# Hymba block on one core: a rule for each product of a head, rotary tables in other buffers, mixes stored from ScalarE's queue, two norm roots moved ahead

## The chip, the cores and the metric

The kernel runs on one core of a Trainium2 chip. A core has five engines with instruction queues of their own: TensorE (PE in the profile, PEld its weight loads), VectorE (DVE), ScalarE (ACT), GpSimd (POOL) and SyncE (SP). In this kernel nearly all transfers between HBM and on-chip memory are issued by SP. The metric is the time of one execution in microseconds of device time, the median of several runs.

## The reference, cut to what matters

One layer over 1040 tokens (16 learned meta tokens and 1024 of input) of width 1024, in float32: a token mixer with eight heads, then a gated MLP with a causal depthwise convolution. Heads 0 to 3 are mLSTM heads (convolved q and k, exponential gates, a carried state), heads 4 to 7 retention heads (rotary q and k, a fixed decay). Each head's output is normalised, gated and projected.

```python
def token_mixer(u, w_in, ml_conv_w, ml_b_i, ml_b_f, ml_norm_g, rt_norm_g, w_out):
    proj = up @ w_in
    (ml_q, ml_k, ml_v, ml_o, ml_i, ml_f, rt_q, rt_k, rt_v, rt_g) = jnp.split(proj, offs, axis=-1)
    qk = jax.nn.silu(causal_dwconv(jnp.concatenate([ml_q, ml_k], axis=-1), ml_conv_w))
...
    h_ml = mlstm_chunkwise(to_chunks(q), to_chunks(k), to_chunks(v),
                           to_chunks(li[..., None])[..., 0], to_chunks(lf[..., None])[..., 0])
    h_ml = head_norm(from_chunks(h_ml), ml_norm_g).reshape(b, lp, ML_HEADS * ML_DV)
    h_ml = jax.nn.sigmoid(ml_o.astype(jnp.float32)) * h_ml
    rq = rotary(rt_q.astype(jnp.float32).reshape(b, lp, RT_HEADS, RT_DQK), pos)
...
    h_rt = retention_chunkwise(to_chunks(rq), to_chunks(rk), to_chunks(rv), log_gamma)
    h_rt = head_norm(from_chunks(h_rt), rt_norm_g).reshape(b, lp, RT_HEADS * RT_DV)
    h_rt = jax.nn.silu(rt_g.astype(jnp.float32)) * h_rt
    mixed = jnp.concatenate([h_ml, h_rt], axis=-1).astype(u.dtype)
    return (mixed @ w_out)[:, n_pad:]

        h = h + token_mixer(rmsnorm(h, norm_mix_g[l]), w_in[l], ml_conv_w[l], ml_b_i[l], ml_b_f[l],
                            ml_norm_g[l], rt_norm_g[l], w_out[l]).astype(h.dtype)
        h = h + channel_mixer(rmsnorm(h, norm_ffn_g[l]), w_up[l], w_gate[l], ffn_conv_w[l],
                              w_down[l]).astype(h.dtype)
    return rmsnorm(h, norm_final_g)[:, N_META:]
```

## The kernel before

**Products.** Activations lie with features on the 128 partitions and tokens along the free side. Every large product is computed with seven block products instead of eight (a Winograd form): `ROWS` lists the seven with the activation block that each uses, "11" to "22" and the sums S1 to S4. Each operand is split into a rounded high half and a low rest (`hi`, `lo`), and three matmuls at the fast float32 format stand for one product (`mm3s`, L858 to L860). So each weight block needs a cast on ACT (L440) and a subtraction on DVE (L445) before PE can use it (`parts`). The sequential part, the scan of a head, uses plain float32 matmuls.

**Start (to about 90 us).** `norm_sums` and `norm_split` normalise the input in five pieces: squares on ACT and DVE, sums on PE (L786), a root on ACT (L788), a reciprocal on DVE (L789), a broadcast on PE (L798), the scaling on DVE (L837) and the split (L838, L842). Meanwhile PE computes v, q and k of head 4 and the gate columns. Then DVE and ACT build S1 to S4 and split them (`usplit`, L1722 and L1723). For S4 the block "12" is first copied by POOL to the tiles `x12` (L1743), since its own place becomes that of S4's low half. `x12` has the tags A1 and A2; the tables of the heads (rotary cosine and sine, or the mLSTM weights) have the same tags, so `tables_load(4)` (L1053, L1054) has to wait until S4 is split.

**The planned stage (about 80 to 720 us).** The program walks through the products of the heads in the order 4, 0, 1, 2, 3, 5, 6, 7: q and k (`qk_steps`), v for pairs of heads (`v_steps`), the output gate (`o_steps`). `slot` emits one step of a product and, between steps, side tasks from the list `side`, in order. Side tasks of a head are the convolution or the rotary turn (`qk_tasks`), the tables (`tables_tasks`), nine pairs of `scan_a` (score product L1465, transposition L1470, then pt on DVE at L1484 or L1489 and kw on ACT at L1481) and `scan_b` (state update u at L1513, output n at L1515, C on DVE, norm statistics), and for three pieces of the tokens `post_steps`: `stats`, and two times `half`, which transposes into the one bank tr (L1573), multiplies into `mx` (L1581) and stores it to `mxd` in HBM from SP (L1594). `mx` has three buffers.

Many tasks are generators: `tick` advances those in `pend` (weights being split) and `front` (side tasks under way), and emits deferred evacuations. A cost model in `watch` keeps a clock for each engine (`load`) and the end of each instruction (`fin`); tasks wait until the model says that their input is ready (`done.can`, `settle`, `landed`). A step emits at most two side tasks, at most one of them with PE work, and none while DVE or ACT is more than 2.5 us ahead of PE in the model; weights up to three units ahead of the running product (`near`) are split first. With `pinned` set, the order written so is the order on PE, DVE and ACT; transfers are placed by the framework's scheduler, which has an estimate of its own.

**Weights.** `jput` loads raw weights from SP as soon as one of four slots is free; a slot is freed when its last block has been split. `w_unit` adds up blocks of the output weights on DVE (L601 to L605) for later; `first_right` reads mixes back from `mxd` and splits them for the first output product.

**Hand-over.** After the last gate product (`o_steps(7)`) the output product `mixw` starts, with its first weights split by `mixw.prep` (L742 on ACT, L743 on DVE), between the last chunks of head 7's scan.

```python
near = [g for g in pend if order.get(owner[id(g)], 10 ** 6) <= cursor[0] + 3]
for q in (near, front, pend):
...
    if q is pend and not rush[0] and max(load["DVE"], load["Activation"]) - load["PE"] > 3:
        break
    if not rush[0] and until[id(g)] > load["PE"] + 0.5:
        continue
```

## Time and profile before

| what | value |
|---|---|
| median of 3 runs (lowest, highest) | 1569.39 us (1566.6, 1570.87) |
| the profiled execution's own time | 1569.85 us |
| its span, first to last instruction | 1567.6 us |
| mean granted clock of PE | 0.984 |
| moved by DMA | 223.80 MB, mean 143 GB/s |

The profile is that of one execution. Its page gives busy times of engines, the span in 40 slices, the DMA queues, the chain of work that ended last, and the costliest groups of instructions. Other views of the same trace list waits (who waited for whom), instructions in order of time, and busy time and granted clock by stretch. An instruction is named by its line in the kernel, its engine and its tiles, output before input; x is a count. Busy time of PE is that of pipelined matmuls whose ends are modelled, so a busy PE is not PE at its peak. "<-" names what ended a wait, inferred from semaphores.

### The profile page before, as it was taken

To read this page: it belongs to the slowest core of one execution; us is meant where nothing else is said; L and a number is where in the kernel's file an instruction comes from. 1 tells how busy PE (TensorE), PEld (TensorE's weight loads), DVE (VectorE), ACT (ScalarE), POOL (GpSimd) and SP (SyncE) were. 2 spreads that over 40 slices of the span, in tenths; PEclk is the share of its full clock that TensorE was granted. 3 is DMA by queue.
4 is the path that set the end of the run, shared out by engine and by line. 5 is a ranking of instruction groups with operands and counts; after the bars stand their busy time and mean duration, and the time that the engine had idled before them with its cause. 6 is when DMAs were issued, how large, how long until landed. Compare 5 with 4: busy or idle time off the path is not lost.

```text
span 1567.6 us, 25461 instructions
## 1 busy us (share of the span) xinstructions
PE 1503.6 (96%) x9929; PEld 1362.7 (87%) x9929; DVE 1092.4 (70%) x2107; ACT 757.7 (48%) x1454; POOL 73.3 (5%) x133
## 2 busy tenths in 40 slices
PE   7979998999999998999999999999999999999997
PEld 6969888899989898997887988999999999888887
DVE  7775677667676767684777778766666666678657
ACT  5355545445555454655344556444444444434443
POOL 1000000000000000000000000222220000000000
PEclk8989999999999999999999999999999999999999
DMA  6022245323632246569542417788873223943313
GB/s 226 1 82 55 81 135 189 108 72 102 191 103 94 89 135 202 171 248 349 201 122 81 148 54 226 215 208 198 210 180 99 77 76 104 387 134 101 97 52 108
DMA packets 104585, 223.80 MB, mean 143 GB/s; under 512 B 10520, under 2 KB 33760, under 8 KB 104288
## 3 DMA queue, kind: packets, MB, share of 16 engines
q1 hardware_dynamic: 95872, 199.02, 38.0%
q0 software_dynamic: 8448, 23.07, 7.3%
q8 instruction: 78, 1.28, 0.3%
q14 instruction: 43, 0.35, 0.1%
q10 hardware_dynamic: 144, 0.07, 0.0%
HBM read 178.05 MB, written 67.15 MB: 156 GB/s over the span
## 4 chain that ended last, share of the span: by engine, by line
PE 87%; DVE 7%; DMA 3%; ACT 2%; issue 1%; SPq 0%; DVEq 0%; ACTq 0%
PE pdx L860 3%; PE pdx L859 3%; PE pdx L858 3%; PE pup_x L859 2%; PE pup_x L860 2%; PE pga_x L858 2%; PE pup_x L858 2%; PE pga_x L859 2%; PE pga_x L860 2%; PE n L1515 2%; PE pdy L860 2%; PE pdy L859 2%; PE pdy L858 2%; PE u L1513 2%; PE pv L898 2%; PE pwx L860 2%
## 5 line engine op out<-in xcount | busy, mean ns | idle before, releaser
L742 ACT CAST hi_up<-raw_up 128x512 fp32r<-128x512 f32 (+1 forms) x52 | 36.4, 719 | 107.1 <-PE pga_z L859 60.6
L743 DVE TENSOR_TENSOR lo_ga<-fraw_ga,hi_ga 128x512 fp32r<-128x512 f32 (+1 forms) x52 | 41.9, 808 | 38.7 <-ACT hi_ga L742 38.6
L858 PE MATMUL pup_x<-uh_g,hi_up 128*128 128x256 f32 (+1 forms) x240 | 67.2, 283 | 1.2 <-ACT uh_g L1857 1.2
L743 DVE TENSOR_TENSOR lo_up<-raw_up,hi_up 128x512 fp32r<-128x512 f32 (+1 forms) x52 | 41.3, 810 | 38.2 <-ACT hi_up L742 37.4
L859 PE MATMUL pup_x<-ul_g,hi_up 128*128 128x256 f32 (+1 forms) x240 | 67.4, 282 | 0.1
L860 PE MATMUL pup_x<-uh_g,lo_up 128*128 128x256 f32 (+1 forms) x240 | 66.4, 282 | 0.0
L743 DVE TENSOR_TENSOR lo_d<-rd,hi_d 128x1024 fp32r<-128x1024 f32 (+1 forms) x34 | 37.7, 1113 | 32.8 <-ACT hi_d L742 32.7
L742 ACT CAST hi_ga<-fraw_ga 128x512 fp32r<-128x512 f32 (+1 forms) x52 | 36.4, 719 | 46.3 <-PE pup_z L859 23.4
L860 PE MATMUL pdx<-uh_d,lo_d 128*128 128x512 f32 (+1 forms) x156 | 57.9, 375 | 0.0
L859 PE MATMUL pdx<-ul_d,hi_d 128*128 128x512 f32 (+1 forms) x156 | 57.8, 374 | 0.0
L742 ACT CAST hi_d<-rd 128x1024 fp32r<-128x1024 f32 (+1 forms) x34 | 32.3, 959 | 49.2 <-PE pdy L859 32.5
L860 PE MATMUL pdy<-uh_d,lo_d 128*128 128x512 f32 x132 | 51.9, 393 | 0.0
L859 PE MATMUL pdy<-ul_d,hi_d 128*128 128x512 f32 x132 | 51.7, 392 | 0.0
L858 PE MATMUL pdx<-uh_d,hi_d 128*128 128x512 f32 (+1 forms) x156 | 48.5, 372 | 0.0
L858 PE MATMUL pdy<-uh_d,hi_d 128*128 128x512 f32 x132 | 47.9, 389 | 0.0
L858 PE MATMUL pga_x<-uh_g,hi_ga 128*128 128x512 f32 x120 | 47.5, 396 | 0.0
L859 PE MATMUL pga_x<-ul_g,hi_ga 128*128 128x512 f32 x120 | 47.5, 396 | 0.0
L858 PEld LDWEIGHTS pup_x<-uh_g,hi_up 128*128 128x128 f32 x240 | 45.3, 189 | 2.3 <-ACT uh_g L1857 1.4
L860 PE MATMUL pga_x<-uh_g,lo_ga 128*128 128x512 f32 x120 | 47.1, 393 | 0.0
L859 PEld LDWEIGHTS pup_x<-ul_g,hi_up 128*128 128x128 f32 x240 | 45.4, 189 | 1.0 <-DVE ul_g L1858 0.3
L860 PEld LDWEIGHTS pup_x<-uh_g,lo_up 128*128 128x128 f32 x240 | 44.8, 189 | 0.8
L1581 DVE SCALAR_TENSOR_TENSOR mx<-tr,vec,sig 128x386 f32<-128x386 f32 (+2 forms) x42 | 24.0, 572 | 26.0 <-PE tr L1573 17.0
(1684 smaller groups left out, 5789.7 us busy)
## 6 DMA issues: line engine op xcount, KB each, us to landing
raw_up<-w_up_d SPq DMA_DIRECT2D x22, 512.0 KB, 4.4
fraw_ga<-w_gate_d SPq DMA_DIRECT2D x22, 512.0 KB, 4.6
acts<-cv SPq DMA_DIRECT2D x44, 256.0 KB, 4.3
wsd<-w_down_d POOLq DMA_DIRECT2D x44, 256.0 KB, 6.3
rd<-wsd SPq DMA_DIRECT2D x22, 512.0 KB, 3.5
raw_w<-w_out_d SPq DMA_DIRECT2D x20, 512.0 KB, 5.1
wsw<-raw_w SPq DMA_DIRECT2D x32, 256.0 KB, 2.1
raw_m<-w_out_d SPq DMA_DIRECT2D x14, 512.0 KB, 3.7
```

The source lines that it names most:

```text
L742: AC.copy(hi[:, o:o + n], x)
L743: V.tensor_tensor(lo[:, o:o + n], x, hi[:, o:o + n].bitcast(F32), ALU.subtract)
L858: m.append(PE.matmul(pt, ah, xh_, start=first and k == 0, stop=False, skip_group_check=True))
L859: PE.matmul(pt, ah, xl_, start=False, stop=False, skip_group_check=True)
L860: m.append(PE.matmul(pt, al, xh_, start=False, stop=last and k == n - 1, skip_group_check=True))
L898: PE.matmul(pv[:, :nv], u[:, kb % 4, j0:j0 + L], (w0hi, w0lo)[j][kb // 4][:, o:o + nv], start=i + j + kb == 0, stop=i == 1 and kb == KB - ...
L1513: PE.matmul(up[:, :nv], kw[:L], v, start=True, stop=True)
L1515: PE.matmul(pn[:L, :nv], pt[:L, :L], v, start=True, stop=c == 0)
L1581: return V.scalar_tensor_tensor(dst, tr[:, x0 - t0:x1 - t0], vec[:, g:g + 1], sig(b, p)[:, x0 - a0:x1 - a0], ALU.mult, ALU.mult)
```

## The change

- **Rules.** A table `RULES` gives each product (kind and head) seven numbers: how many units ahead weights count as near; how far ahead of PE a generator's input may be; at what lead of DVE or ACT the rest of `pend` pauses; the same limit for side tasks; how many of these in a step; which of three orders the queues have; how many of them may have PE work. `RULE` holds for the others. Side tasks that start on PE go to a new queue, `hot`.
- **Model.** A DMA from ACT is priced apart from SP's; a change between the two matmul formats costs 0.1 in the model; `done["tr"]` is set after the mix has been emitted and not before; `scan_a` waits for the one before it, `scan_b` for the evacuation of its values; the stage starts with DVE 7.0 and ACT 5.5 behind, before 4.0 and 2.0.
- **Tables.** `x12` takes the tags v2 and v3; `tables_load(4)` stands ahead of the copies and of S4.
- **Stores.** `half` stores the mix from ACT's queue, after `settle`; `first_right` waits until all three pieces of its mix are stored.
- **Memsets.** The ones in `mv`, `den` and `vz` are written by POOL, in `scan_a` of the first chunk.
- **Norms.** Squares and casts are ordered behind the last root, and a sum behind the last reciprocal.
- **Hand-over.** `mixw.pump` and `mixw.prep(0)` come before the last steps of `o_steps(7)`; the next `prep` after the first quarter of each product.

```diff
+RULE = (3, 0.5, 3.0, 2.5, 2, 0, 1)
+RULES = {
+    ("o", 0): (4, 0.3, 3.0, 2.5, 2, 0, 3),
+    ("o", 1): (3, 0.0, 2.0, 1.5, 2, 1, 3),
...
+    ("vp", 2): (3, 0.3, 3.0, 4.0, 2, 1, 2),
+}
...
-            load[eng] = t + 0.4
+            load[eng] = t + (0.4 if eng == "SP" else 0.1)
...
+                whole = F32 in [x.dtype for x in ins.ins]
+                c += 0.1 * (whole != kindof[0])
+                kindof[0] = whole
...
-        near = [g for g in pend if order.get(owner[id(g)], 10 ** 6) <= cursor[0] + 3]
-        for q in (near, front, pend):
+        near = [g for g in pend if rank.get(owner[id(g)], 10 ** 6) <= cursor[0] + rule[0][0]]
+        for q in ((hot, near, front, pend), (near, hot, front, pend), (hot, front, near, pend))[rule[0][5]]:
...
-                if q is pend and not rush[0] and max(load["DVE"], load["Activation"]) - load["PE"] > 3:
+                if q is pend and not rush[0] and max(load["DVE"], load["Activation"]) - load["PE"] > rule[0][2]:
                     break
-                if not rush[0] and until[id(g)] > load["PE"] + 0.5:
+                if not rush[0] and until[id(g)] > load["PE"] + rule[0][1]:
                     continue
...
             def g():
+                while not {(k, x) for x in range(3)} <= stored:
+                    yield
                 ask([i])
...
-        V.reciprocal(col[:, :ns], col[:, :ns])
+        last["recip"] = V.reciprocal(col[:, :ns], col[:, :ns])
...
-        AC.activation(sq[0], xs[0], AF.Square)
+        m = AC.activation(sq[0], xs[0], AF.Square)
+        if r:
+            after(m, last["sqrt"])
...
-            AC.activation(sq[1], xs[1], AF.Square)
+            after(AC.activation(sq[1], xs[1], AF.Square), last["sqrt"])
...
-            V.tensor_tensor(sq[0], sq[0], sq[1], ALU.add)
+            m = V.tensor_tensor(sq[0], sq[0], sq[1], ALU.add)
+            if r:
+                after(m, last["recip"])
...
-            AC.copy(w0hi[i], w0raw[i])
+            after(AC.copy(w0hi[i], w0raw[i]), last["sqrt"])
...
+        if c == 0:
+            mv = mxp.tile([P, 4, 2], F32, tag="mv", name=f"mv{h}_0", bufs=4)
+            den = mxp.tile([P, NCH], F32, tag="den", name=f"den{h}", bufs=2)
+            G.memset(mv[:, 0, :], 1.0)
+            G.memset(den[:, 0:1], 1.0)
+            if h < H:
+                G.memset(vz[:META, VZ[h] * 264 + DV:VZ[h] * 264 + VW], 1.0)
+            firsts[h] = mv, den
...
-                V.memset(mv[:, 0, :], 1.0)
-                V.memset(state["den"][:, 0:1], 1.0)
-                if h < H:
-                    V.memset(vz[:META, VZ[h] * 264 + DV:VZ[h] * 264 + VW], 1.0)
...
+            done.discard("tr")
             tr = ps.tile([P, 512], F32, tag="tr", name=f"tr{h}_{p}_{b}")
...
-            done["tr"] = fin[0] + 0.05
...
             mix_into(mx[:, :w], a0, t1)
+            done.add("tr")
             e = min(t1, MB + HB)
-            nc.sync.dma_start(mxd[i][:, a0 - MA:e - MA], mx[:, :e - a0])
             if e < t1:
                 V.tensor_copy(mm[:, i], mx[:, e - a0:w])
                 posted.add(i)
+            yield from settle()
+            AC.dma_start(mxd[i][:, a0 - MA:e - MA], mx[:, :e - a0])
+            stored.add((i, p))
...
-            return lambda: done.can(("qk", h, int(c > 4)), *([("tab", h)] if h < H else ["gates"] if h == 4 else [])) and not (h == 7 and "meta" in done)
+            return lambda: done.can(*([("pre", h, c - 1)] if c else []), ("qk", h, int(c > 4)), *([("tab", h)] if h < H else ["gates"] if h == 4 else [])) and not (h == 7 and "meta" in done)
...
-            spawn(g, front)
+            spawn(g, hot if pe else front)
...
+        if key:
+            rule[0] = RULES.get(key[:2], RULE)
+        lim, most = rule[0][3:5]
+        pe = max(pe, rule[0][6])
...
-    x12 = [st.tile([P, 2 * SB], F32, tag=f"A{i + 1}", name=f"s4_{i}").rearrange("p (k j) -> p k j", k=2) for i in range(2)]
+    x12 = [vslot(2 + i, f"s4_{i}").rearrange("p (k j) -> p k j", k=2) for i in range(2)]
+    tables_load(4)
     for i in range(2):
         G.tensor_copy(x12[i], part("12", i))
     s1[:] = x12
     need(("o", 4, 1))
     usplit("S4", "S1", "uh2", "ul2")
-    tables_load(4)
...
-    load.update({"DVE": 4.0, "Activation": 2.0})
+    load.update({"DVE": 7.0, "Activation": 5.5})
...
-    go(steps[4:])
+    go(steps[4:12])
+    issue(len(units) - len(fu))
+    while ("o", 7, 6) not in done:
+        slot(steps[10 + used[0]])
+        used[0] += 1
+    mixw.pump()
+    mixw.prep(0)
+    go(steps[12 + used[0]:])
...
     for t in range(KW - 2):
-        for u in (t, t + 1):
-            mixw.prep(u)
+        mixw.prep(t)
         for j in range(4):
             slot(lambda: mixw.mms(t, js=(j,)))
+            if j == 0:
+                mixw.prep(t + 1)
```

More of the change, by code (lines that the diff above doesn't have):

```diff
@@ L133, in watch @@
         if dma:
[L134 removed]
+            load[eng] = t + (0.4 if eng == "SP" else 0.1)
             size = n * o.ap[0][1] * 4e-6
[L136 to L137 removed]
+            if eng == "SP":
+                load["wire"] = max(load["wire"], t + 1.8) + size / 0.3 * (2 if "scr" in str(rd) else 1)
+                end = load["wire"]
+            else:
+                load["wire"] += size / 0.3
+                end = t + 1.8 + size / 0.15
         else:
@@ L340, in body @@
     front = []
+    hot = []
     evacs = []
@@ L345, in body @@
     cursor = [0]
+    rule = [RULE]
     def spawn(g, q=pend, key=None):
@@ L363, in tick @@
     def tick():
-        assert pend or evacs or front
+        assert pend or evacs or front or hot
         fin[0] = 0.0
@@ L410, in flush @@
         rush[0] = True
-        while pend or evacs or front:
+        while pend or evacs or front or hot:
             tick()
@@ L455, in issue @@
             ready[u[0]] = u[2]()
-    order = {}
+    order, rank = {}, {}
     place = {}
@@ L463, in need @@
             order.update({u[0]: i for i, u in enumerate(units)})
-        i = i0 = cursor[0] = order[key]
+            rank.update({k: i for i, k in enumerate(u[0] for u in units if u[1])})
+        i = i0 = order[key]
+        cursor[0] = rank[key]
         if ahead is None:
@@ L1018, in step, with out @@
                     bank = bank.rearrange("p (c j) -> p c j", j=DV)
-                    defer(lambda: evac(n, d, bank))
+                    f, half = QUAD[n]
+                    key = ("v", (a, b)[f], half) if cp == 3 and n in (1, 4, 5, 6) else None
+                    def out():
+                        evac(n, d, bank)
+                        if key:
+                            done.add(key)
+                    defer(out)
                 step.key = "vp", p, n
@@ L1500, in scan_b @@
         if slot == 0:
-            mv = mxp.tile([P, 4, 2], F32, tag="mv", name=f"mv{h}_{p}", bufs=4)
             if p == 0:
-                state["den"] = mxp.tile([P, NCH], F32, tag="den", name=f"den{h}", bufs=2)
-                V.memset(mv[:, 0, :], 1.0)
-                V.memset(state["den"][:, 0:1], 1.0)
-                if h < H:
-                    V.memset(vz[:META, VZ[h] * 264 + DV:VZ[h] * 264 + VW], 1.0)
+                mv, state["den"] = firsts.pop(h)
+            else:
+                mv = mxp.tile([P, 4, 2], F32, tag="mv", name=f"mv{h}_{p}", bufs=4)
             outs[p] = ([], mv, state["den"])
@@ L1603, in ra @@
         def ra(c):
-            return lambda: done.can(("qk", h, int(c > 4)), *([("tab", h)] if h < H else ["gates"] if h == 4 else [])) and not (h == 7 and "meta" in done)
+            return lambda: done.can(*([("pre", h, c - 1)] if c else []), ("qk", h, int(c > 4)), *([("tab", h)] if h < H else ["gates"] if h == 4 else [])) and not (h == 7 and "meta" in done)
         turn = [("vm", p, s) for p, x in enumerate(PAIRS) for s in range(2) if x[s] == h]
         def rb(c):
-            return lambda: (h, c) in pre and done.can(("pre", h, c), *(turn if c == 0 else [("n", h, c - 1)]))
+            v = [("v", h, int(c > 4))] if h not in (4, 7) else []
+            return lambda: (h, c) in pre and done.can(("pre", h, c), *(turn if c == 0 else [("n", h, c - 1)] + v))
         A = [(lambda c=c: scan_a(h, c), 1, ra(c)) for c in range(NCH)]
```

19 lines of the change are left out of this document (10 added, 9 removed), and 16 rows, old and new, of the table RULES.

## The prediction

> **What bounds the kernel now.** The page comes first: the span, the engines' shares and part 4, the chain that ended last (PE is TensorE, PEld its weight load, DVE VectorE, ACT ScalarE, POOL GpSimd).
>
> ```profile
> span 1567.6 us, 25461 instructions
> ...
> PE 1503.6 (96%) x9929; PEld 1362.7 (87%) x9929; DVE 1092.4 (70%) x2107; ACT 757.7 (48%) x1454; POOL 73.3 (5%) x133
> ...
> PE 87%; DVE 7%; DMA 3%; ACT 2%; issue 1%; SPq 0%; DVEq 0%; ACTq 0%
> ```
>
> PE is the bound: it holds 87% of the chain, and the change removes no product. What can be won is where PE stood still (1567.6 - 1503.6 = 64 us) or ran at a low clock. The next view is the busy time in stretches; columns are the stretch, its length, busy PE, PEld, DVE, ACT and POOL, the granted clock, the DMA share and GB/s.
>
> ```profile
> 80.00:120.00 40.00, 29.79 (x228) 27.99 (x229) 29.07 (x73) 20.82 (x41) 0.21 (x2) 0.87 0.25 82
> 120.00:720.00 600.00, 572.94 (x4405) 539.20 (x4404) 409.47 (x938) 310.46 (x652) 8.91 (x42) 0.98 0.43 139
> 720.00:760.00 40.00, 36.29 (x167) 28.00 (x166) 25.45 (x47) 19.99 (x30) 0.00 (x0) 1.00 0.88 329
> ```
>
> Three stretches matter beside the norms at the front: the start of the first gate product (80 to 120; PE idle 10.2 us), the planned stage (120 to 720; idle 27.1 us), and its hand-over to the output product (720 to 760; idle 3.7 us). The change touches nothing behind. DVE is busy 68% of the planned stage (409.47 of 600), so it is late in places and not short as a whole. The list of PE's waits says for whom (total us, times, longest):
>
> ```profile
> PE po4y L858 <- DVE sig L930: 8.4, 1, 8.4
> ...
> PE s L1465 <- DVE pt L1489: 6.4, 2, 4.1
> PE u L1513 <- DVE vz L1507: 6.2, 4, 3.0
> PE tr L1573 <- DVE mx L1581: 4.8, 6, 1.8
> PE po1y L860 <- DVE lo_o L445: 2.9, 1, 2.9
> ...
> PE po1x L860 <- DVE lo_o L445: 1.8, 1, 1.8
> ```
>
> Each long wait is also followed by PE at half clock for some microseconds. The same view of stretches, cut around the dips:
>
> ```profile
> 24.00:36.00 12.00, 10.16 (x50) 10.08 (x50) 11.88 (x30) 5.26 (x10) 0.00 (x0) 0.58 0.15 57
> 92.00:108.00 16.00, 9.05 (x55) 8.84 (x56) 11.48 (x33) 11.67 (x20) 0.00 (x0) 0.68 0.20 71
> 196.00:208.00 12.00, 9.02 (x45) 7.31 (x45) 9.53 (x21) 4.73 (x11) 0.18 (x1) 0.72 0.52 176
> ...
> 372.00:380.00 8.00, 8.00 (x53) 7.52 (x53) 7.12 (x12) 2.74 (x6) 0.17 (x1) 0.79 0.19 68
> ```
>
> Length times (1 - clock) is what a dip takes: 5.0, 5.1, 3.4 and 1.7 us; in the second, half falls into the idle time itself, so I count 2.6.
>
> **The change part by part.**
>
> *Rotary tables in free buffers.* The copies of x12 leave the tiles A1 and A2 for v2 and v3, and the loads of the tables come ahead of them. The timeline of DVE, SP's queue and PE (start, length, instruction, count, and in brackets the idle time before it and what ended that):
>
> ```profile
> 74.09 2.43 DVE L1723 TENSOR_TENSOR uS1l<-s,uS1h 128x1056 fp32r<-128x1056 f32 x2 [0.81 <-ACT uS1h L1722]
> ...
> 83.86 2.42 DVE L1723 TENSOR_TENSOR uS4l<-s,uS4h 128x1056 fp32r<-128x1056 f32 x2
> ...
> 86.15 0.38 SPq L1053 DMA_DIRECT2D A<-rot_d  x1
> ...
> 91.55 0.71 DVE L1131 TENSOR_TENSOR qT<-rawq,A 128x528 f32<-128x528 f32 x1 [5.27 <-DMA A<-rot_d]
> ...
> 94.38 0.71 DVE L1132 TENSOR_TENSOR kT<-kT,A 128x528 f32<-128x528 f32 x1 [2.12 <-DMA A<-rot_d]
> ...
> 98.95 0.58 PE L858 MATMUL po4y<-uS1h,hi_o 128*128 128x256 f32 x1 [8.38 <-DVE sig L930]
> ```
>
> The tables now go out at 86.15, when the split of S4 has read A1 and A2; DVE's first rotary product waits 5.27 us for one and 2.12 us for the other, the sum into sig stands behind it in DVE's order, and PE needs that bank: 8.38 us idle. In the new kernel A1 and A2 are free when S1 has been split (74.09 + 2.43 = 76.5); at the measured pace (86.15 to 94.38 for both) the tables land by 84.8, before DVE is through with S4 (86.3). The wait goes. Upper bound 8.4 + 2.6 = 11 us; lower bound DVE's own 5.27 + 2.12 = 7.4, since DVE is then the late one. I take -9. Late next is DVE, with the gate arithmetic; the planner is told so (DVE 7 us behind, not 4). SP now holds these two loads until 76.5, and the weight loads queued behind them on SP want slots that come free no earlier. POOL's two copies go into tiles whose last reader, the value product of the last chunk, is through before S1 is split, so S4 comes no later. If SP's order put the tables behind those weight loads, a part of the wait would stay.
>
> *Roots of two norms ahead.* In the timeline ACT takes the first block's root (9.78) behind a cast of value weights, the second's (18.44) behind two squares:
>
> ```profile
> 8.80 1.07 ACT L865 CAST w0hik<-w0raw 128x1056 fp32r<-128x1056 f32 x1 [0.29 <-DMA w0raw<-w_v_d]
> 9.78 0.26 ACT L788 ACTIVATE rcola<-pca,vec 128x2 f32<-128x2 f32 x1
> ...
> 16.53 1.06 ACT L815 ACTIVATE sqr<-x 128x1024 f32<-128x1024 f32 x1
> 17.50 1.04 ACT L821 ACTIVATE sqr<-x 128x1024 f32<-128x1024 f32 x1
> ...
> 18.44 0.24 ACT L788 ACTIVATE rcola<-pca,vec 128x1 f32<-128x1 f32 x1
> ...
> 26.42 1.25 PE L898 MATMUL pv<-w0hiq,u11h 128*128 128x264 f32 x4 [1.83 <-ACT u11h L838]
> ```
>
> Ahead of them the first comes up to 1.0 us earlier and the second up to 2.1; the casts that now wait for the first root are needed only by the product behind it. Bounds: nothing (DVE is busy 11.88 of the 12 us that follow), and 1.0, PE's wait of 1.83 and the dip's 5.0, together 7.8. I take -2, nearest to the waits themselves.
>
> *Memsets to POOL.* Of ones in mv, den and vz:
>
> ```profile
> 200.04 0.06 DVE L1507 MEMSET vz<- 16x1 f32 x1
> ...
> 200.17 1.22 PE L1513 MATMUL u<-vz,kw 16*128 16x257 f32 x2 [2.98 <-DVE vz L1507]
> ...
> 117.13 0.10 POOL L998 MEMSET v<- 128x4 f32 x1 [38.21 <-ACT gates L1221]
> ```
>
> The write takes 0.06 us, but DVE had no idle time ahead of it: it stands at the end of a backlog, and PE waits for it at four heads, 6.2 us. On POOL (0.10 us each, an idle engine) and one task earlier it is done before anyone asks; there it waits for the last reader of vz, and behind it stand only copies of den, which are read a piece later. Bounds: nothing, if PE runs into the same backlog at its next use of DVE, to 6.2 with two dips of 3.4 and 1.7, 11.3. I take -4: two thirds of the wait, no dip. The Trainium skill, "TensorE: Matmul & The Clock Gate", section "Part 1: The HAM clock gate (the "warmup" mystery)", has the clock halve only after an idle window of about 3.4 us. Here a wait of 2.98 was enough, so the trace does not bear the rule out; by the rule the upper bound would be 6.2.
>
> *Scores, queue and rules.* Scan tasks that start on PE get a queue of their own, ahead; a score product is no longer emitted before the planner has the last one read out (pt); each product has seven numbers of its own (how far ahead weights are split, when side work pauses, how many tasks per step). These reorder the same instructions. What they aim at is 6.4 us for pt (upper bound 8.1 with one dip like the last row's, 1.7), and 9.1 us for weight halves, of which 2.9 and 1.8 stand above (12.5 with two dips of 1.7). Lower bound: an order that is worse by as much. I take -3 and -3, a third to a half, since the planner's clock is a model and DVE stays as loaded.
>
> *Fewer turns.* Up to three PE side tasks now go together. What a turn costs shows in PE's timeline, merged rows left out:
>
> ```profile
> 453.91 0.31 PE L1470 MATMUL s<-cs,kT 128*128 128x128 f32 x1
> 453.97 0.37 PE L858 MATMUL po3y<-uS4h,hi_o 128*128 128x258 f32 x1
> 454.18 0.28 PE L859 MATMUL po3y<-uS4l,hi_o 128*128 128x258 f32 x1
> 454.30 0.28 PE L860 MATMUL po3y<-uS4h,lo_o 128*128 128x258 f32 x1
> ```
>
> The first main product behind a score takes 0.21 us to the next start, not 0.12: 0.09 a turn. The code has 8 x (9 + 9 + 6) = 192 such tasks, 17 us in all; if a third join another, -6. I take -3, between nothing and -9.
>
> *Stores of the mixes on ACT's queue.* This line's own rows, minimum, median and maximum in ns, then one issue from ACT:
>
> ```profile
> L1594 SPq DMA_DIRECT2D mxd<-mx x42: 319/326/840, 165.5 to 676.4; - x42
> ...
>   DVE mx L1581: 5.4, 6
> ...
> 0.74 0.43 ACTq L239 DMA_DIRECT2D vec<-vecs_d  x1
> ```
>
> SP no longer stands still for a mix with weight loads queued behind it. In return ACT issues 42 transfers of 0.43 us, 18 us on an engine that is 52% busy there (310.46 of 600), and what waits behind each is a cast of weights or an evacuation that PE needs. Issue alone: +1, by half of it falling on idle ACT and a small part of the rest on PE; bounds 0 and +9. The 4.8 us for tr hang on mx, which waits 5.4 us for old stores; with tr now marked free only after its read: -1.5, bounds 0 and -4.8. The Trainium skill, "DMA: Bandwidth & Descriptors", section "Issuing engines are not separate DMA queues", says that transfers from either queue run on the same 16 engines and interleave. By it the 5.4 us stay, and this sum would be -0.5 instead of -1.5; no row here shows a store from ACT.
>
> *First output weights split early.* prep(0) stands ahead of the last steps of head 7:
>
> ```profile
> 721.85 0.50 PE L858 MATMUL pwx<-wone,hi_w 128*128 128x512 f32 x1 [1.46 <-ACT hi_w L742]
> 723.11 0.50 PE L860 MATMUL pwx<-wone,lo_w 128*128 128x512 f32 x1 [0.52 <-DVE lo_w L743]
> ```
>
> 1.46 + 0.52: -2, bounds 0 and -3.3 with the two shorter waits of 736 to 740. The waits added for the values' evacuation and for complete mixes only hold back tasks in the planner; I cost them at nothing, hidden behind PE's main products, with a wait like 4.1 us if one is forced.
>
> Sum: -9 - 2 - 4 - 3 - 3 - 3 + 1 - 1.5 - 2 = -26.5. The profiled execution took 1569.85 us (2.25 around its span), 0.46 above the median of 1569.39: 1543.35, or 1542.9 at the median. I say 1543.
>
> **The rivals.**
>
> *Only the fixed edits count.* The waits of the planned stage move to the next use of a late DVE; tables, norms and end remain: -9 - 2 - 2 = -13, 1556. For it: behind the wait at 200.17 lies a real backlog. Against it: 32% of DVE is idle there.
>
> *Slower: ACT blocked by its stores.* A store on ACT waits for DVE's mix, and casts stand behind it. The planner delays the store until it believes the mix done; DVE is up to 3 us later than believed (the wait of 2.98). It decides from 27.5 / 42 = 0.65 us per store that reaches PE, the sum without its +1 over the stores. At 1 us: 1569.4 - 27.5 + 42 = 1584. Against it: PE's waits name ACT for few us today.
>
> *All of it.* Every named wait goes with its dip: -11 - 7.8 - 11.3 - 8.1 - 12.5 - 4.8 - 3.3 = -59. With the ends whole (-22.1), half of the planned stage's (-18.4) and the turns at -5 it is -45.5: 1524. For it: each wait has an edit aimed at it. Against it: a late DVE is late for whoever comes next.
>
> *It does not do what it says*: the tile framework's own scheduler orders loads by its estimate, tables still late, and the planned order merely different: 1569.
>
> **How the numbers follow.** Forecast (1534 to 1553) 0.54; fixed edits only (1553 to 1563) 0.20; everything (below 1534) 0.13; no effect 0.04; slower 0.09. The range 1529 to 1562 holds the forecast, most of the second and a third of the third. 0.3% is 4.7 us, about what this measurement can tell from no change: faster 0.87, same 0.04, slower 0.09.
>
> **What would show it.** DVE's first rotary product has no DMA wait, and PE no idle time over 3 us between 86 and 110. The second block's root lies ahead of the squares, and the dip at 24 to 36 is shorter. No PE wait names vz; those on pt fall below 3 us. PE's idle time from 120 to 720 is 12 to 20 us instead of 27.1. No wait for hi_w ahead of the first output product. I am wrong if waits on ACT's casts, behind stores, come up among PE's longest, or if PE's idle time there stays at 27.

## The result, and the profile after

| kernel | median (lowest, highest) | runs | profiled span |
|---|---|---|---|
| before | 1570.13 us (1566.6, 1571.55) | 4 | 1567.6 us |
| changed | 1527.86 us (1527.2, 1529.32) | 4 | 1525.4 us |

The ratio is 0.9735, with a 95% interval of 0.9717 to 0.9754: the change takes 42 us away. Forecast were 1543 us and a range of 1529 to 1562, so the gain was larger than the sum said, and the time came out just below the range. One execution is left out in what follows: a fourth one of e14_old_hand_over took 5160.98 us, where the other three took about 1529, and what slowed it is not known.

The page of the changed kernel, its span, part 1 and the chain by engine:

```profile
span 1525.4 us, 25488 instructions
...
PE 1489.9 (98%) x9929; PEld 1350.0 (88%) x9929; DVE 1090.1 (71%) x2087; ACT 755.6 (50%) x1453; POOL 73.6 (5%) x153
...
PE 89%; DVE 6%; DMA 2%; ACT 2%; issue 1%; SPq 0%; DVEq 0%; ACTq 0%
```

The same 9929 products, 13.7 us less of busy PE and 28.5 us less of PE standing still (1525.4 - 1489.9 = 35.5, before 64). DVE has as much to do as before. The stretches of the changed kernel, columns as in the prediction:

```profile
80.00:120.00 40.00, 38.61 (x315) 36.04 (x314) 30.89 (x81) 22.01 (x45) 0.32 (x3) 1.00 0.34 83
120.00:680.00 560.00, 553.61 (x4323) 522.17 (x4322) 403.32 (x907) 307.11 (x646) 8.81 (x55) 1.00 0.45 149
680.00:720.00 40.00, 36.53 (x157) 28.47 (x156) 23.86 (x47) 18.63 (x29) 0.00 (x0) 0.91 0.83 306
```

Equal clock times hold different work in the two kernels, so the planned stage is better cut at the same two products: from head 0's first query product to the first output product. Before, and then changed:

```profile
113.40:721.90 608.50, 579.97 (x4457) 545.46 (x4457) 415.74 (x962) 316.25 (x666) 9.12 (x44) 0.98 0.42 138
```

```profile
100.30:675.20 574.90, 568.51 (x4447) 536.50 (x4447) 415.76 (x942) 311.10 (x657) 9.13 (x58) 1.00 0.44 144
```

This pair answers most of the question. The stage begins 13.1 us earlier (113.4 to 100.3), is 33.6 us shorter, and what follows is 4.5 us longer, partly since more of the last head's scan now lies behind its end, partly by two new waits, for wr, that the list below has: 42.2 in all, the difference of the spans. Of the 33.6, 22.1 are PE's idle time (28.5 before, 6.4 now) and 11.5 its busy time. Most of the latter are dips of the clock: at a granted clock of 0.50 the stage ran for 20.5 us before (6.8 us from 199.9, and 3.4 us each from 275.0, 350.1, 374.0 and 612.9) and runs for 3.4 us now (from 123.7), and half of the difference is 8.5 us. That leaves 3 us for all else, fewer turns among it. DVE's busy time is the same to 0.02 us. Nothing was taken off the engine that PE waited for; its work was put in another order.

The list of PE's waits, changed kernel (total us, times, longest):

```profile
PE s L1523 <- DVE pt L1547: 2.6, 1, 2.6
PE pwy L901 <- DVE wr L1288: 1.8, 1, 1.8
...
PE u L1568 <- DVE C L1581: 1.5, 2, 0.9
PE tr L1629 <- DVE mx L1637: 1.5, 3, 1.1
PE pwy L900 <- ACT wr L1288: 1.3, 1, 1.3
```

The 8.4 us for sig, the 6.2 for vz and both waits for weight halves are gone. Of the 6.4 us for pt, 2.6 are left, of the 4.8 for tr, 1.5. New are the two waits for wr, behind the hand-over.

### The profile page after: what moved, and what is told of

It is laid out like the page before. It is cut to its first block, busy times and chain, and to the rows that moved or that the text cites. A ratio compares the mean times of both kernels' runs of the same rounds, so it can differ in the third digit from the quotient of the medians.

```text
span 1525.4 us, 25488 instructions
## 1 busy us (share of the span) xinstructions
PE 1489.9 (98%) x9929; PEld 1350.0 (88%) x9929; DVE 1090.1 (71%) x2087; ACT 755.6 (50%) x1453; POOL 73.6 (5%) x153
## 4 chain that ended last, share of the span: by engine, by line
PE 89%; DVE 6%; DMA 2%; ACT 2%; issue 1%; SPq 0%; DVEq 0%; ACTq 0%
PE pdx L902 3%; PE pdx L901 3%; PE pdx L900 3%; PE pup_x L901 2%; PE pup_x L902 2%; PE pga_x L900 2%; PE pup_x L900 2%; PE pga_x L901 2%; PE pga_x L902 2%; PE pdy L902 2%; PE pdy L901 2%; PE pdy L900 2%; PE n L1570 2%; PE pwx L902 2%; PE u L1568 2%; PE pv L940 2%
## 5 line engine op out<-in xcount | busy, mean ns | idle before, releaser
L780 ACT CAST hi_ga<-fraw_ga 128x512 fp32r<-128x512 f32 (+1 forms) x52 | 36.4, 719 | 45.3 <-PE pup_z L901 21.9
```

Of the source, the lines that this page charges most:

```text
L780: AC.copy(hi[:, o:o + n], x)
```

## The experiments

Differences among versions of the changed kernel are taken from their medians: it gave the same time in two sets of runs (1527.86 and 1527.74), while the kernel before spread from 1565 to 1578 over all. An experiment that undoes an edit and becomes slower by x shows that the edit is worth x among the others, as long as nothing else changes with it. The planner, though, makes its order anew for each kernel. In the planned stage the order of DVE's and ACT's instructions is that of the kernel compared with in e4, e8 and e12, and in e14 up to its last 10 us. In e2 and e3 it is not: about 80 of DVE's instructions stand elsewhere in e2 and about 40 in e3. What these two cost is thus the price of the edit together with that of another order.

The table sets the experiments side by side; "against changed" is the difference from 1527.86, and idle is that of PE in the planned stage, cut as above (6.4 in the changed kernel, 28.5 in the one before).

| kernel | median us | against changed | idle us |
|---|---|---|---|
| e5_again | 1527.74 | -0.1 | 6.3 |
| e1_one_rule | 1544.33 | +16.5 | 22.6 |
| e6_no_hot | 1544.99 | +17.1 | 21.9 |
| e7_no_chain | 1534.03 | +6.2 | 10.4 |
| e9_fixed_only | 1547.95 | +20.1 | 20.0 |
| e13_wide_rule | 1549.9 | +22.0 | 23.7 |
| e11_one_task | 1535.9 | +8.0 | 13.8 |
| e2_memsets_dve | 1536.72 | +8.9 | 11.8 |
| e3_stores_sp | 1532.81 | +5.0 | 10.0 |
| e8_old_norms | 1525.72 | -2.1 | 6.4 |
| e12_first_root | 1523.67 | -4.2 | 6.8 |
| e14_old_hand_over | 1528.6 | +0.7 | 9.0 |
| e4_only_tables | 1565.01 | | 28.8 |
| e10_order_only | 1555.43 | | 21.9 |

**The tables alone (e4_only_tables)**, in the kernel before:

```diff
-    x12 = [st.tile([P, 2 * SB], F32, tag=f"A{i + 1}", name=f"s4_{i}").rearrange("p (k j) -> p k j", k=2) for i in range(2)]
+    x12 = [vslot(2 + i, f"s4_{i}").rearrange("p (k j) -> p k j", k=2) for i in range(2)]
+    tables_load(4)
...
     usplit("S4", "S1", "uh2", "ul2")
-    tables_load(4)
```

> The kernel before with the tables alone in free buffers and loaded early; nothing else changed. PE's bound: 11 us faster, 1559, with neither the wait of 8.4 us nor the clock dip at 92. VectorE's bound: 7.4 us faster, 1563, with a new wait of PE of 1 to 4 us between 86 and 110. If the loads are late for another reason: 1568 to 1570.

Measured: 1565.01 us over ten runs against 1573.36, ratio 0.9948 (0.9926 to 0.997): 8 us. In its timeline the load goes out 12 us earlier than at 86.15, and DVE's first rotary product stands in no wait for it:

```profile
73.57 0.33 SPq L1053 DMA_DIRECT2D A<-rot_d  x1
...
82.76 0.70 DVE L1131 TENSOR_TENSOR qT<-rawq,A 128x528 f32<-128x528 f32 x1
```

PE's wait of 8.4 us for sig is down to 0.8, and the planned stage begins 9.9 us earlier. The step is right in mechanism and, as far as the interval tells (5 to 12 us), in size.

**The rules (e1_one_rule), the queue ahead (e6_no_hot), the order of score products (e7_no_chain)**, each undone alone, and all three together (e9_fixed_only, which leaves the fixed edits):

```diff
-RULES = {
...
-}
+RULES = {}
```

> The changed kernel with an empty table of rules: every product has the default rule, all else stays. Theory R (the seven numbers of each product bring most of the planned stage's gain): 15 to 20 us come back, 1543 to 1548, and PE's idle time from 120 to the output product rises from about 7 to over 18 us. Rival F (memsets, queue hot, the wait of a score for the last pt and the stores each take their own wait away, whatever the numbers): at most 5 us come back, under 1533.

```diff
-            spawn(g, hot if pe else front)
+            spawn(g, front)
```

> The changed kernel with side tasks that start on PE put back into the common queue; the rules stay. Theory R (the numbers do it, the queue is one of the things they order): 2 to 6 us slower than the changed kernel, waits on pt or C come up. Theory H (the queue ahead is what took the 6.4 us of pt away): 6 to 10 us slower, waits on pt over 5 us. If it is without effect: within 1 us.

```diff
-            return lambda: done.can(*([("pre", h, c - 1)] if c else []), ("qk", h, int(c > 4)), *([("tab", h)] if h < H else ["gates"] if h == 4 else [])) and not (h == 7 and "meta" in done)
+            return lambda: done.can(("qk", h, int(c > 4)), *([("tab", h)] if h < H else ["gates"] if h == 4 else [])) and not (h == 7 and "meta" in done)
```

> The changed kernel where a score product no longer waits, in the planner, for the pt before it. If this condition took the waits on pt away: 4 to 8 us slower, with a wait on pt over 3 us. If the rules order it anyway: within 2 us.

> The changed kernel with one rule for all products, no queue of its own for scan tasks and no wait of a score for the last pt: tables, memsets, stores, norms, hand-over and the new planner's model stay. Theory A (the parts add up, each takes its own waits away): 14 to 20 us faster than before, about 1553, the rest being the order's. Theory M (the numbers suit only the kernel that they stand in, so that every part taken out alone cost more than it is worth): 25 us or more faster than before, under 1547.

Measured: e1 1544.33 (ratio 0.9814, 0.9768 to 0.9861), e6 1544.99 (0.9831, 0.9798 to 0.9865), e7 1534.03 (0.9762, 0.9722 to 0.9802), e9 1547.95 (0.9862, 0.9837 to 0.9886). The planned stage of e1, e6 and e9, cut at the same two products:

```profile
99.00:695.10 596.10, 573.50 (x4447) 540.27 (x4448) 418.44 (x953) 314.41 (x659) 9.39 (x58) 0.99 0.42 139
```

```profile
100.80:698.40 597.60, 575.66 (x4446) 539.38 (x4446) 415.87 (x942) 308.79 (x656) 10.07 (x58) 0.99 0.42 138
```

```profile
100.10:704.00 603.90, 583.94 (x4463) 548.61 (x4464) 420.47 (x957) 316.83 (x668) 8.87 (x58) 0.98 0.42 139
```

Idle time of PE is length less its busy time: 22.6, 21.9 and 20.0 us, against 6.4 with all of it. DVE is as busy in e6 as in the changed kernel, to 0.1 us. Which wait comes back differs. PE's waits of e1, e6 and e7:

```profile
PE tr L1609 <- DVE mx L1617: 9.9, 7, 3.6
...
PE pq0x L880 <- DVE sig L952: 2.8, 2, 2.4
PE po6x L882 <- DVE lo_o L459: 2.0, 1, 2.0
```

```profile
PE s L1523 <- DVE pt L1547: 8.4, 5, 5.1
...
PE pm L600 <- DMA raw_m<-w_out_d: 4.8, 1, 4.8
PE tr L1629 <- DVE mx L1637: 3.0, 6, 1.0
```

```profile
PE s L1523 <- DVE pt L1542: 4.1, 4, 1.6
PE s L1523 <- DVE pt L1547: 3.9, 3, 2.8
```

Without the rules PE waits for mixes and weight halves, without the queue ahead and without the chain for pt. Rules and queue do not add up: 16.5 and 17.1 apart, but 20.1 together with the chain. Each is nearly worthless without the other: with the chain, the rules alone bring 3.0 us over e9 and the queue alone 3.6. Why is not shown; that the rules were chosen for a plan with the queue would fit. Of the forecasts, e1's theory R came in and e7 cost what was said, by waits of 2.8 us at most; e6 cost more than either of its theories gave it, and e9, 21.0 us faster than the kernel before, lies between A and M.

**Is it the numbers by product, or only more tasks in a step (e13_wide_rule)?** One rule for all, with three tasks in a step, as six of the table's rows have:

```diff
-RULE = (3, 0.5, 3.0, 2.5, 2, 0, 1)
-RULES = {
...
-}
+RULE = (3, 0.5, 3.0, 2.5, 3, 0, 3)
+RULES = {}
```

> The changed kernel with one rule for all products, the default with up to three tasks a step, all of them allowed PE work (3, 0.5, 3.0, 2.5, 3, 0, 3). If the number of tasks is what the rules bring: within 4 us of the changed kernel, under 1532, with about 150 visits or fewer. If it takes numbers found for each product: 10 us or more slower, over 1538.

Measured: 1549.9 us (ratio 0.9846, 0.9814 to 0.9879), 5.6 slower than e1 with the old single rule. Its planned stage:

```profile
99.50:707.90 608.40, 584.66 (x4484) 549.23 (x4485) 421.31 (x969) 317.93 (x674) 10.27 (x58) 0.98 0.43 140
```

PE idles 23.7 us. A visit is a stretch of side products (tiles s, u, n, tr and v) between two main ones; counted in PE's timelines there are 174 in the planned stage before, 135 in the changed kernel, and 127 here, the fewest. Fewest turns and nearly the slowest version: turns are not where the time went.

**The turns (e11_one_task).** The last number of every rule set to 1:

```diff
-    ("o", 0): (4, 0.3, 3.0, 2.5, 2, 0, 3),
+    ("o", 0): (4, 0.3, 3.0, 2.5, 2, 0, 1),
...
-    ("vp", 2): (3, 0.3, 3.0, 4.0, 2, 1, 2),
+    ("vp", 2): (3, 0.3, 3.0, 4.0, 2, 1, 1),
```

> The changed kernel with the last number of each rule at 1: one PE side task a step. If fewer turns between the two matmul formats are worth what the prediction gave them: 3 to 5 us slower from turns alone, about 180 visits instead of 149. If the later scan also brings waits: 8 us or more. If the model would have put them side by side anyway: within 1 us.

Measured: 1535.9 us (ratio 0.979, 0.9765 to 0.9815), 8.0 slower. From 100 to 700 us it has 178 visits where the changed kernel has 146; 32 times the 0.09 us of the prediction would be 2.9. Its planned stage does not show them:

```profile
101.10:684.30 583.20, 569.37 (x4447) 536.61 (x4447) 418.76 (x942) 311.93 (x658) 11.14 (x58) 1.00 0.43 142
```

PE's busy time is 0.86 us above the 568.51 of the changed kernel, with 170 visits in the stage against 135: 0.02 us each. (One stretch of 3.4 us at half clock lies in either.) The idle time is 7.4 us longer. So the 8.0 us are waits, of which PE's list shows the mixes and a weight half again:

```profile
PE tr L1629 <- DVE mx L1637: 3.4, 4, 1.3
PE po6x L902 <- DVE lo_o L479: 2.0, 1, 2.0
```

The experiment does not isolate the turn, since taking tasks apart also moves what DVE gets when; but it leaves no room for 3 us of turns.

**The memsets (e2_memsets_dve)** back on DVE, in `scan_b`:

```diff
-            G.memset(mv[:, 0, :], 1.0)
-            G.memset(den[:, 0:1], 1.0)
-            if h < H:
-                G.memset(vz[:META, VZ[h] * 264 + DV:VZ[h] * 264 + VW], 1.0)
...
+                V.memset(mv[:, 0, :], 1.0)
+                V.memset(state["den"][:, 0:1], 1.0)
+                if h < H:
+                    V.memset(vz[:META, VZ[h] * 264 + DV:VZ[h] * 264 + VW], 1.0)
```

> The changed kernel with the three memsets back on VectorE, at their old place. Theory F: the waits on vz come back, 6.2 us and up to 11.3 with their clock dips, 1534 to 1539. Theory R: the planned order no longer has a backlog there, so less than 3 us come back, under 1531.

Measured: 1536.72 us (ratio 0.9768, 0.9732 to 0.9804), 8.9 slower, for 20 writes of 0.06 us. The wait for vz is back, if smaller than before, and a weight half is late too:

```profile
PE u L1568 <- DVE vz L1560: 2.6, 3, 1.6
...
PE po3y L902 <- DVE lo_o L479: 2.3, 1, 2.3
...
PE pm L600 <- DVE vz L915: 1.3, 1, 1.3
```

PE idles 5.4 us more, and two stretches of 3.4 us at half clock are new (from 345.3, behind a wait for vz, and from 420.4, at the wait for lo_o), 1.7 us each: 8.8 in all. Theory F came in by its time, but not all of it by its waits: that for vz is 3.9 us, and the late weight half belongs to the other order.

**The stores (e3_stores_sp)** back on SP:

```diff
-            AC.dma_start(mxd[i][:, a0 - MA:e - MA], mx[:, :e - a0])
+            nc.sync.dma_start(mxd[i][:, a0 - MA:e - MA], mx[:, :e - a0])
```

> The changed kernel with the mixes stored from SyncE again. If SyncE standing still for a mix was what made weights late: 3 to 8 us slower, 1531 to 1536, with waits on weight halves. If the stores cost ScalarE more than they save SyncE: 1 us faster or the same, 1526 to 1528.

Measured: 1532.81 us (ratio 0.974, 0.9704 to 0.9776), 5.0 slower. The waits of SP's queue, e3:

```profile
SPq L1655 <- DVE mx L1637: 80.7, 20, 36.2
```

In the kernel before this row has 75.3 us in 21 waits. In the changed kernel it does not exist. But this time is not won. Without the stores SP stands as long at the next thing, a free slot for weights, here in e3 and then in the changed kernel:

```profile
SPq L328 <- DVE lo_vp L479: 40.6, 9, 7.2
```

```profile
SPq L328 <- DVE lo_vp L479: 95.7, 9, 39.4
```

All of SP's waits from 100 to 700 us come to 513 us in e3 and to 521 in the changed kernel. Nor do weights come later in e3: ACT's longest waits for their loads are 4.8 and 2.9 us there, 5.1 and 2.6 in the changed kernel. Waits on weight halves did come, as the expectation has it (2.3 and 0.9 us, for lo_o), but from DVE's order. The changed kernel, then e3:

```profile
247.04 0.69 DVE L479 TENSOR_TENSOR lo_o<-raw_o1a,hi_o 128x512 fp32r<-128x512 f32 x1
...
252.58 0.75 DVE L972 TENSOR_TENSOR sig<-sig,po1y 128x258 f32<-128x258 f32 x2
```

```profile
250.17 0.42 DVE L972 TENSOR_TENSOR sig<-sig,po1y 128x258 f32<-128x258 f32 x1 [1.76 <-PE po1y L902]
...
251.93 0.68 DVE L479 TENSOR_TENSOR lo_o<-raw_o1a,hi_o 128x512 fp32r<-128x512 f32 x1
...
258.09 0.39 PE L902 MATMUL po1y<-uS1h,lo_o 128*128 128x258 f32 x1 [2.33 <-DVE lo_o L479]
```

In e3 the sums into sig stand ahead of the weight half and wait for PE, and the weight halves behind them are late; the load of that block went out at 232.48. The planner prices an issue on the two queues differently (0.4 and 0.1 us), which may be why its order came out another. So the 5.0 us are those of a plan with the stores on SP against a plan with them on ACT. What the queue alone is worth, no run shows.

What the stores cost in the changed kernel is seen by the line's own rows, with those who waited for the issue:

```profile
L1655 ACTq DMA_DIRECT2D mxd<-mx x42: 326/326/387, 150.6 to 633.3; - x42
...
  ACT hi_o L474: 5.1, 1
  ACT hi_vp L474: 2.8, 1
  DVE mx L1637: 1.9, 2
```

An issue on ACT takes 0.326 us, as on SP, and not the 0.43 of the one row that the prediction had. By these rows ACT is held twice, 7.9 us in all, but the timeline has another cause. The cast waits for a block that DVE is still adding up, and starts when that ends:

```profile
403.26 0.69 DVE L566 TENSOR_TENSOR raw_o3a<-raw_o3a,raw_o3b 128x512 f32<-128x512 f32 x1
...
404.04 0.62 ACT L474 CAST hi_o<-raw_o3a 128x512 fp32r<-128x512 f32 x1 [5.09 <-DMA mxd<-mx]
```

It is the same with hi_vp at 473.19. No PE wait of the planned stage names an ACT cast; DVE's wait for old stores falls from 5.4 to 1.9 us. The rival in which ACT's stores make the kernel slower is out.

**The norms (e8_old_norms: all their orders undone; e12_first_root: all but the two casts behind the first root):**

```diff
-        m = AC.activation(sq[0], xs[0], AF.Square)
-        if r:
-            after(m, last["sqrt"])
+        AC.activation(sq[0], xs[0], AF.Square)
...
-            after(AC.activation(sq[1], xs[1], AF.Square), last["sqrt"])
+            AC.activation(sq[1], xs[1], AF.Square)
...
-            m = V.tensor_tensor(sq[0], sq[0], sq[1], ALU.add)
-            if r:
-                after(m, last["recip"])
+            V.tensor_tensor(sq[0], sq[0], sq[1], ALU.add)
...
-            after(AC.copy(w0hi[i], w0raw[i]), last["sqrt"])
+            AC.copy(w0hi[i], w0raw[i])
```

The last two lines are in e8 alone.

> The changed kernel with squares, casts and sums of the norms in the old order. If the early roots are worth what the prediction gave them: 2 us slower. If the 2 us by which the first gate product starts earlier come from another part (the copies of x12, the clock): within 0.7 us, and the gate product of head 4 starts at 76 us here too.

> The changed kernel with only the first of the two norm orders (the casts of value weights behind the first root); squares and sums as before. If the later squares are what made the new order 2 us slower: 1 us faster than with both old orders, 1524.5. If the casts are: no faster than the changed kernel, 1527.5.

Measured: e8 1525.72 us (ratio 0.9708, 0.9676 to 0.9741), 2.0 faster than the changed kernel on the same chip (e5, 1527.74); e12 1523.67 us (0.9712, 0.9682 to 0.9741), 4.2 faster and the best version found. ACT and PE in the changed kernel's timeline, then in e12's:

```profile
17.50 0.26 ACT L826 ACTIVATE rcola<-pca,vec 128x1 f32<-128x1 f32 x1 [1.84 <-PE pca L824]
17.66 1.05 ACT L853 ACTIVATE sqr<-x 128x1024 f32<-128x1024 f32 x1
...
27.88 1.08 PE L940 MATMUL pv<-w0hiq,u11h 128*128 128x264 f32 x4 [0.93 <-ACT u11h L880]
```

```profile
15.64 1.05 ACT L853 ACTIVATE sqr<-x 128x1024 f32<-128x1024 f32 x1
...
17.56 0.26 ACT L826 ACTIVATE rcola<-pca,vec 128x1 f32<-128x1 f32 x1
...
26.13 0.75 PE L936 MATMUL pv<-w0hiq,u11h 128*128 128x264 f32 x4
```

The root comes at the same time in both; the order bought it nothing, because its sums come no earlier. The squares that were held back for it start 2.0 us later, and with them the product that needs the next norm, by 1.75. The other half, the first root ahead of the casts, is worth the 2.0 us between e8 and e12; they ran on two chips and their ranges overlap, so its size is uncertain. Neither forecast for e8 came in; e12 came out as the first of its two has it.

**The hand-over (e14_old_hand_over)** as before:

```diff
-    go(steps[4:12])
-    issue(len(units) - len(fu))
-    while ("o", 7, 6) not in done:
-        slot(steps[10 + used[0]])
-        used[0] += 1
-    mixw.pump()
-    mixw.prep(0)
-    go(steps[12 + used[0]:])
+    go(steps[4:])
...
+    issue(len(units) - len(fu))
     flush()
     mixing[0] = False
+    mixw.pump()
...
-        mixw.prep(t)
+        for u in (t, t + 1):
+            mixw.prep(u)
```

> The changed kernel with the hand-over to the output product as before. If the early split is worth what the prediction gave it: 2 us slower, 1530, with a wait on hi_w and none on wr. If the wait on wr at 708 with its clock dip is its price: no slower, 1525 to 1528. If it carries more than was priced: over 1532.

Measured: 1527.45, 1528.6 and 1530.2 us (ratio 0.9716, 0.9684 to 0.9748). Their median is 0.7 over the changed kernel, less than the spread of either: no gain can be told. Its waits show why:

```profile
PE pwx L900 <- ACT hi_w L780: 3.4, 1, 3.4
```

The changed kernel trades these 3.4 us for the 1.8 and 1.3 us on wr in its own list above.

**The order alone (e10_order_only).** The mirror of e9: rules, queue, chain and the planner's prices stay, the fixed edits (tables, memsets, stores, norms, hand-over, and the 4.0 and 2.0 of the start) are as before. Three of the edits, the others being those above:

```diff
-    tables_load(4)
     for i in range(2):
...
     usplit("S4", "S1", "uh2", "ul2")
+    tables_load(4)
...
-    load.update({"DVE": 7.0, "Activation": 5.5})
+    load.update({"DVE": 4.0, "Activation": 2.0})
...
-            AC.dma_start(mxd[i][:, a0 - MA:e - MA], mx[:, :e - a0])
+            nc.sync.dma_start(mxd[i][:, a0 - MA:e - MA], mx[:, :e - a0])
```

> The other half: rules, queue hot, the wait of a score and the new planner's model stay; tables, memsets, stores, norms and hand-over are as before. Theory A: 22 to 28 us faster than before, about 1545, so that both halves together make the 42 us. Theory M: less than 12 us faster, over 1558.

Measured: 1555.43 us (ratio 0.9908, 0.988 to 0.9937), 13.5 below the 1568.97 of before on that chip. There e9, the fixed edits alone, is 21.0 below. Neither of the theories came in; 13.5 lies between them. Together the halves make 34.5, less than the whole change: each is worth some 7 us more with the other in place (41.1 lie between 1568.97 and the changed kernel's 1527.86). The intervals are about 4 us either way for each half, so that by the times alone this is uncertain; PE's idle time in the planned stage says the same more clearly: of 28.5 us the fixed edits alone take 8.5, the order alone 6.6, and both 22.1. The planner's prices stand in both halves, and no run takes them out. PE's waits of e10 have what each fixed edit removes:

```profile
PE po4y L896 <- DVE gsm L1207: 5.4, 1, 5.4
PE u L1564 <- DVE vz L1556: 5.0, 4, 1.6
PE pwx L896 <- ACT hi_w L780: 3.4, 1, 3.4
```

**The changed kernel again (e5_again)**, to see how far one execution stands for the others:

> The changed kernel unchanged, to have its time on the chip on which the next three run: 1527 to 1530 us. Its profile tells what differs from one execution to the next: the clock dips, if their length hangs on a window that is not tied to the kernel, differ by steps of about 1.7 us at the same waits.

Measured: 1527.74 us (1526.66 to 1529.26; ratio 0.9723, 0.9689 to 0.9756).

## Why the prediction fell short

| step | predicted us | measured us | by |
|---|---|---|---|
| tables | -9 | -8 | e4 |
| norms | -2 | +2 | e8 |
| memsets | -4 | -9, with another order | e2 |
| stores on ACT | +1 | -5, with another order | e3 |
| tr free after its read | -1.5 | in no run by itself | |
| hand-over | -2 | -1, not told from 0 | e14 |
| these together | -17.5 | -21, with the planner's prices | e9 |
| scores, queue, rules, turns | -9 | -20 on top of them, -13.5 alone | e9, e10 |
| sum | -26.5 | -42 | |

The rows from e2 to e14 are worth what they are in the presence of the rest, so they need not add up to e9's.

- **The step that failed** is "I take -3 and -3, a third to a half, since the planner's clock is a model and DVE stays as loaded". DVE did stay as loaded (415.74 and 415.76 us), and that was no reason: the stage lost 22.1 of its 28.5 us of idle time, and some of its dips. Idle time of 12 to 20 us was forecast for 120 to 720; it is 560 - 553.61 and 40 - 36.53, together 9.9. DVE, busy 68% of the stage before and 72% of it now, had slack enough to be on time nearly everywhere. That the waits' total was the term's upper bound was written down (8.1 and 12.5, with their dips); the discount on it had no row behind it. Nor does the order take away only the waits that it was priced for: with the rules out (e1) the largest that comes back is for mixes, 9.9 us.
- **Tables**: right by mechanism, place and size. The wait for the load is gone, no wait over 3 us is left in that stretch (PE idles 1.4 us from 80 to 120, before 10.2), and the stage begins 13.1 us earlier, 9.9 of them by this edit in e4.
- **Norms**: wrong sign. The prediction had the second root up to 2.1 us earlier because its squares stood ahead of it on ACT. It came 0.94 us earlier (18.44 to 17.50), and e12 has it at 17.56 without the order: it waits for its sums on PE, not for ACT. The price of the order, squares late for the next norm, was not costed: of a step that is moved, what now stands behind is the first thing to price. The dip from 24 to 36 is shorter, as forecast, but e12, without this order, has none there.
- **Memsets**: right mechanism, and too small. With the writes on DVE, PE waits 3.9 us for vz, about the 4 forecast; but "no dip" did not hold, since one of the two dips in e2 follows such a wait. The rest of the 9 is the other order's, so the term's own size stays open.
- **Stores**: the term of ACT was too high by a duration (0.43 instead of 0.326 us) and by the casts behind the stores, of which none reached PE. The path that the prediction names in favour of the edit and does not price, "SP no longer stands still for a mix with weight loads queued behind it", is not the cause that e3 shows: SP stands as long without the stores, and the late weight halves of e3 come from DVE's order. That e3 fell into its forecast of 3 to 8 us was luck. The Trainium skill, "DMA: Bandwidth & Descriptors", section "Issuing engines are not separate DMA queues", says that a second issuing engine saves only the issue time of the sequencer. No run here speaks against it: an issue takes 0.326 us on either queue, and the loads of weights are waited for no longer in e3.
- **Turns**: 39 fewer visits in the planned stage would be 3.5 us at 0.09 us each, and the dips leave about 3 us of the lost busy time. But e11, with 35 visits more than the changed kernel, has only 0.86 us more busy time. So 3 us is the most that turns can have given; that they gave it is not borne out.
- **Hand-over**: the wait for hi_w is gone, as forecast; the new waits on wr, which were not, take most of it back.
- **Rivals**: what came in is "All of it", at 1524 us with a chance of 0.13. Its objection, "a late DVE is late for whoever comes next", is what e9 shows of the fixed edits by themselves (idle time still 20.0 us), and the whole does not bear it out. That the time itself was met is partly luck: this rival had 22.1 us at the ends and 23.4 in the planned stage with the turns, and they are 8.6 and 33.6. "Only the fixed edits" gave 1556; e9 gives 1547.95.

What stays open: which of the nineteen rules carry the gain. Only all of them, none, one in their place, and all with their last number at 1 were run. What the planner's prices, the stores' queue and the memsets are worth with the order held fast, no run shows. And that each half is worth more beside the other is seen in the idle time, but no run separates it by edit.

## What to carry to other kernels

When the bound engine waits in many small places for a helper that is busy two thirds of the time, look at the order first: here 22.1 of 28.5 us of such idle time went without taking work off the helper. Price the waits in full with their clock dips, and keep the discount for waits whose helper has no slack. Undo edits in both directions (each out of the new kernel, and the group into the old one), since orders that were made for each other are worth little apart. Where a planner makes the order, compare the order of the instructions in both traces before a difference in time is put down to the edit: e2 and e3 look like tests of one edit and are not. And a queue's waits are a cost only if what stands behind them is late: SP's 75 us at the stores went over to its next wait.

## What the runs showed of the chip

**The same kernel dips differently from one execution to the next.** Stretches of the changed kernel and of its second profile (e5), over the same work at the front:

```profile
24.00:36.00 12.00, 9.86 (x68) 9.58 (x66) 11.63 (x28) 6.79 (x10) 0.09 (x1) 0.86 0.15 57
```

```profile
24.00:36.00 12.00, 10.37 (x60) 9.38 (x60) 11.17 (x28) 6.79 (x10) 0.09 (x1) 0.72 0.16 62
```

The granted clock is the third number from the right: 12 x 0.14 = 1.7 us are lost in one and 12 x 0.28 = 3.4 in the other; the kernel before lost 5.0 there, e12 none. Losses come in steps of 1.7 us: in the stretches named above, the granted clock is 0.50 for 3.4 us or 6.8 us on end. The Trainium skill, "TensorE: Matmul & The Clock Gate", section "Part 1: The HAM clock gate (the "warmup" mystery)", has half the clock after windows of about 3.4 us that run freely, so that a kernel's count of slow products differs from run to run. The steps agree: half of 3.4 is 1.7. So a dip seen in one profile is a matter of one to three such steps and not a fixed price.

**A kernel with fewer waits also repeats better.** The eight runs of the changed kernel lie within 2.7 us; the kernel before, over more runs and chips, spreads over 13, and over 11.4 in seven runs on one chip (1564.85 to 1576.29). That its more frequent waits, each a chance of a dip, are the reason fits with the above but was not tested.
